# Compressed path's copies in single steps, the window keys' splits behind its hidden layer, early rotations two steps later, priority for two sums of every group

## The chip, the core and the metric

The kernel runs on one core of a Trainium2 chip. The core has five engines that run side by side, each with an instruction queue of its own: TensorE (PE in the profile; its weight loads are PEld), VectorE (DVE), ScalarE (ACT), GpSimd (POOL) and SyncE (SP), which here only issues transfers. Work passes between two on-chip memories, SBUF and PSUM (where matmuls accumulate, in banks of 512 float32 columns), and DRAM. The metric is the device time of one execution in microseconds, the median over several runs.

## What is computed

One layer of a decoder trunk on 512 tokens of width 1024. A wide projection feeds two token mixers: a causal pooling mixer over four window sizes, and sparse attention with 16 heads in 2 key groups and three branches (compressed keys, selected blocks, sliding window). With 512 tokens all blocks are selected and the window covers everything, so that two branches are plain causal attention with keys and values of their own. Two gates merge the mixers, an output projection and a residual follow, then a squared-ReLU MLP (1024 to 4096 to 1024), a residual and a norm. Cut to what matters here:

```python
h = rms_norm(x, norm_mix)
u, q, kc, vc, ks, vs, kw, vw, g_nsa, g_merge = split(h @ w_in)
q, ks, kw = apply_rope(q), apply_rope(ks), apply_rope(kw)
k_cmp = apply_rope(compress(kc, pe_k, w_ck1, w_ck2))
v_cmp = compress(vc, pe_v, w_cv1, w_cv2)
# compress: blocks of 32 tokens, every 16, plus pe; gelu(flat @ w1) @ w2
o = g0 * attend(q, k_cmp, v_cmp) + g1 * attend(q, ks, vs) + g2 * attend(q, kw, vw)
merged = sigmoid(g_a) * (pool_mixer(u) @ w_proj_pool) + sigmoid(g_b) * (o @ w_proj_nsa)
x = x + merged @ w_out
x = x + square(relu(rms_norm(x, norm_mlp) @ w_ff1)) @ w_ff2
out = rms_norm(x, norm_final)
```

## The kernel before

**Split products.** Every float32 matrix is held as a high and a low part (type fp32r in the profile). ScalarE copies the raw matrix into the high part, VectorE subtracts that from the raw matrix for the low part. A product is three matmuls: high by high, high by low, low by high. So each weight, once its transfer has landed, takes a ScalarE copy (line 475, or 366 in the MLP) and a VectorE subtraction (478, or 371) before TensorE can use it. The weight's name in the profile is `raw`, then `wh` and `wl` (`w3h` and `w3l`, `wkt`).

**Order.** The program is emitted in one order by Python code; a planner then sets the order of each engine's queue, with durations of its own. Of the instructions that it reckons ready at a moment, it takes the one emitted first. `tc.high_priority(n)` counts an instruction as emitted n places earlier. `behind(x)` keeps an instruction behind x on its engine. On the chip each engine follows its queue in the planned order; `raw` buffers, weight slots and PSUM banks are reused in turn.

**Steps.** TensorE's work is the backbone: `for k in P1` in the first phase goes through the columns of the input projection in the order `ck ks u0 wk0 u1 wk1 u2 wk2 kw wk3 cv V0 V1 V2 wv0 u3 wv1 q0 ...`, ending with `q2 pp0 pp1 pp2 pp3`. Each key's matmuls come in pieces. After each piece stand `ahead()`, which emits the next half of the next weight's two copies where a slot is free, and one yield. At each yield `run` calls `step_side`, which lets every generator in the queue `side` go on by one step. These side generators hold what follows a product on the other engines:

- `cmp_first` (line 893): copies the projection of the compressed keys or values (`ck`, `cv`) into an interleaved table on ScalarE (896, 897, twice each), adds the position rows (904) and makes the split table `cA` (907, 908). It is a plain function, called at the end of `cv`.
- `cmp_mlp1` (923) multiplies `cA` with the first compress weights. `cmp_rest` follows: gelu by a tanh (934 to 943), some empty steps, two transposes on TensorE (957), the copy `cg` on ScalarE with 60 places of priority (960), and the second weights on TensorE (969).
- `rope` (810): ScalarE takes the product out of PSUM (816), four transfers of 64 KB exchange the halves (`rs<-rx`, 819), then come empty steps, four products (836), two sums (829), one step each, and then `done`. In the attention phase the products run on GpSimd instead, in given places.
- `k_done` (849): splits rotated keys into `KH` and `KL` for each key group, four copies and two more on ScalarE (855, 859), two subtractions on VectorE (857). `k_done(0)` belongs to `ks`, `k_done(1)` to `kw`. `q_done` (865) does it for a pair of heads (867 to 871).
- `project_v` (the keys V0, V1, V2) multiplies the value and gate columns into four banks `psV`, in three pieces of the depth, four token tiles each; when it is done, ScalarE and VectorE copy the four banks out (1048 to 1050).
- `token_sums`, `pool_mix` and others run beside these.

**Groups.** The gate of mixer A, and the MLP's first layer, are computed with seven products in place of eight (Strassen's scheme): class `Group`, order A11, S3, S1, S2, A12, A22, S4 (the first MLP chunk in another order). `main` makes the combinations on VectorE: `u2 = s - b` (610), `u3 = c + u2` (611), `u3 = d + u3` (614). A22 goes on accumulating in the bank of c, which 611 must have read. Line 611's instruction is `roots`, behind which every weight subtraction of line 371 that is emitted later is kept.

Of the kernel before, what the change touches and what calls it, by code (L numbers as in the profile page):

```python
# [62 lines left out]
def trunk(ctx: ExitStack, tc: tile.TileContext, A, out):  # L63
# [507 lines left out]
    class Group:  # L571
# [29 lines left out]
        def main(self):  # L601
            while "A11" not in self.done:
                yield
            ACT.activation(self.s, self.ps["a"], AF.Copy)
            self.done.add("s")
            while not {"S1", "S2", "S3"} <= self.done:
                yield
            yield
            with tc.high_priority(60) if self.key[0] == "G" else nullcontext():
                DVE.tensor_tensor(self.u2, self.s, self.ps["b"], op=ALU.subtract)  # L610
                roots[:] = [DVE.tensor_tensor(self.u3, self.ps["c"], self.u2, op=ALU.add)]
            self.done.add("u3")
            yield
            DVE.tensor_tensor(self.u3, self.ps["d"], self.u3, op=ALU.add)
            self.done.add("u2")
            yield from self.act(self.u3, 1, 1)
# [107 lines left out]
    def behind(made):  # L724
        return tc.issue_after(made.ins)
# [3 lines left out]
    def sums0(i):  # L729
        junk = p0.tile([128, D], F32, tag="junk", bufs=1, name="junk")  # L730
        ACT.activation(junk, xt[i], AF.Square, accum_out=rr[i][:, 0:1])
        r = ACT.activation(rr[i][:, 1:2], rr[i][:, 0:1], AF.Sqrt, bias=eps_t, scale=1.0 / D)
        DVE.reciprocal(rr[i][:, 2:3], rr[i][:, 1:2])
        for h in range(2):
            c = slice(512 * h, 512 * h + 512)
            v = DVE.scalar_tensor_tensor(xt[i][:, c], xt[i][:, c], rr[i][:, 2:3], psg[h], op0=ALU.mult, op1=ALU.mult)
        return r, v
# [9 lines left out]
    def evac0(i, after=None):  # L747
        sl = slice(128 * i, 128 * i + 128)
        for a in range(2):
            ks = slice(4 * a, 4 * a + 4)  # L750
            r = ACT.activation(hT[0][:, ks, sl], trs[i][a], AF.Copy)
            with behind(after) if after else nullcontext():
                v = DVE.tensor_tensor(hT[1][:, ks, sl], trs[i][a], hT[0][:, ks, sl].bitcast(F32), op=ALU.subtract)
        for a in range(2 if i > 1 else 0):
            c = 128 * (i - 2)
            ACT.activation(quarter(MAf, 2 * a + 1)[:, :, c:c + 128], trs[i][a], AF.Copy)
        return r, v
# [8 lines left out]
    r, _ = evac0(1)  # L766
    with behind(r):
        r, _ = sums0(2)
# [4 lines left out]
    with behind(conv[0]):  # L773
        r, v = sums0(3)
    mode["first"] = None
    first_posts = []
# [29 lines left out]
    scored = {"pairs": 0, "rope": 0}  # L806
# [3 lines left out]
    def rope(ps, scale, done, after=0):  # L810

        assert not scored["rope"]
        scored["rope"] = 1
        xr = ap.tile([128, S], F32, tag="rx", bufs=1, name="rx")
        sw = ap.tile([128, S], F32, tag="rs", bufs=1, name="rs")
        ACT.activation(xr, ps, AF.Copy, scale=scale)
        for b in range(4):
            a = b ^ 1
            nc.sync.dma_start(sw[32 * b:32 * b + 32, :], xr[32 * a:32 * a + 32, :])
        yield  # L820
        eng = POOL if mode["pool"] else DVE
        hs = [slice(0, S // 2), slice(S // 2, S)]
        in_slots = mode["pool"]
        for _ in range(4 if in_slots else 2):
            yield

        def add(c):
            with behind(slot["low"]) if in_slots else nullcontext():
                DVE.tensor_tensor(xr[:, c], xr[:, c], sw[:, c], op=ALU.add)

        for c in hs:
            for t, table in ((xr, cosT), (sw, sinT)):
                while in_slots and not slot["long"]:
                    yield
                with behind(slot["scaled"]) if in_slots else nullcontext():
                    eng.tensor_tensor(t[:, c], t[:, c], table[:, c], op=ALU.mult)
                yield
            if c is hs[0]:
                continue
            add(hs[0])  # L840
            yield
            add(hs[1])
        while scored["pairs"] < after:
            yield
        for _ in done(xr):
            yield
        scored["rope"] = 0

    def k_done(br):
        def done(k):  # L850
            for g in range(2):
                r = [slice(64 * h, 64 * h + 64) for h in range(2)]
                src = k[r[g], :].rearrange("p (a b) -> p a b", a=4)
                for h in range(2):
                    ACT.activation(KH[g][r[h], :, br, :], src, AF.Copy)
                yield
                DVE.tensor_tensor(KL[g][r[g], :, br, :], src, KH[g][r[g], :, br, :].bitcast(F32), op=ALU.subtract)
                yield
                ACT.activation(KL[g][r[1 - g], :, br, :], KL[g][r[g], :, br, :].bitcast(F32), AF.Copy)
        return done  # L860
# [14 lines left out]
    with ExitStack() as c1:  # L875
# [15 lines left out]
        def cmp_first(kv):  # L891

            def post(ps):
                kc = scratch[:, 0:1024].rearrange("p (g t) -> p g t", g=2)
                for g in range(2):
                    ACT.activation(kc[0:64, g, :], ps[64 * g:64 * g + 64, :], AF.Copy)
                    ACT.activation(kc[64:128, g, 0:S - 1], ps[64 * g:64 * g + 64, 1:S], AF.Copy)
                a = scratch[:, 1024:2048].rearrange("p (j n) -> p j n", j=16)
                POOL.memset(a[:, :, 31:64:32], 0.0)
                o = 0 if kv == "k" else 16  # L900
                for g in range(2):
                    v = bass.AP(tensor=kc.tensor, offset=kc[:, g, :].offset,
                                ap=[list(kc.ap[0]), [2, 16], [16, 31]])
                    DVE.tensor_tensor(a[:, :, 32 * g:32 * g + 31], v,
                                      pec[:, o:o + 16, None].to_broadcast([128, 16, 31]), op=ALU.add)
                t = p1.tile([128, 16, 128], FR, tag="cA", bufs=1, name="cA")
                DVE.tensor_copy(t[:, :, 0:64], a)
                cA_low.append(DVE.tensor_tensor(t[:, :, 64:128], a, t[:, :, 0:64].bitcast(F32), op=ALU.subtract))
                cA[kv] = t
            return post  # L910

        cA, cA_low = {}, []
# [3 lines left out]
        def cmp_mlp1(kv, i):  # L916
            if i == 0:
                cps[kv] = ps1.tile([128, 256], F32, tag="V", bufs=4, name="psC1")
            ps = cps[kv]
            wH, wL = use(f"w{kv}{i}")  # L920
            for k in range(4):
                for w in (wH, wL):
                    PE.matmul(ps, cA[kv][:, 4 * i + k, :], w[:, k, :], start=i == 0 and k == 0 and w is wH,  # L923
                              stop=i == 3 and k == 3 and w is wL, skip_group_check=True)
            ahead()
            yield
            ahead()
            if i == 3:
                side.append(cmp_rest(kv, ps))

        def cmp_rest(kv, ps):
# [26 lines left out]
            gt = p1.tile([128, 2, 64], F32, tag="cg", bufs=2, name="cg")  # L958
            with tc.high_priority(60):
                ACT.activation(gt, pt, AF.Copy, scale=0.5)  # L960
            yield
            yield
            pm = ps1.tile([128, 2, 64], F32, tag="M", bufs=2, name="psM")
# [148 lines left out]
        def gates(g):  # L1112
# [5 lines left out]
            own = [pair(gate_f[0], i) for i in range(4)]  # L1118
            return Group(f"G{g}", sums_of.get, lambda: ps1.tile([128, S], F32, tag="V", bufs=4, name="psV"), own, act)

        first_posts += [cmp_first("k"), lambda ps: rope(ps, -0.125, k_done(0))]
        pr = ps1.tile([128, 36], F32, tag="M", bufs=2, name="psM")
        PE.transpose(pr, rows, ident[0:36, 0:36])
        DVE.tensor_copy(pec, pr)
# [55 lines left out]
    with ExitStack() as c2:  # L1180
# [304 lines left out]
        ps = ps2.tile([128, S], F32, tag="T", bufs=T_BANKS, name="psT")  # L1485
# [489 lines left out]
    ps = whole.ps["d"][0]  # L1975
# [13 lines left out]
    ps = whole.ps["d"][1]  # L1989
# [27 lines left out]
```

## Time and profile before

| | |
|---|---|
| median of 3 runs | 776.96 us (776.59 to 777.86) |
| the profiled execution | 777.74 us |
| its span, first to last instruction | 775.9 us |
| matmuls (PE instructions) | 4675 |
| DMA moved | 146.55 MB |

The span runs in four parts: the projections and the mixers' inputs up to about 165 us, attention to about 370, the output projections to about 440, and the MLP. Times in a timeline count from the start of the span. In a row of the timeline stand the start, the length, the engine, the line in the kernel, the operation, what is written and read with its shape, the count of merged instructions, and in brackets how long the engine was idle before it and what ended that. In the list of waits stand who waited for whom, the total, the count and the longest, in us. The releaser is inferred, and where an instruction waits for several things it is the one that came last by the profile.

### The profile page before, as it was taken

What the parts mean: (1) busy time and instruction counts of PE and PEld (TensorE: products, weight loads), DVE (VectorE), ACT (ScalarE), POOL (GpSimd) and SP (SyncE); (2) the same over time, 40 slices, a digit from 0 to 9 for tenths busy, and PEclk for the clock granted to TensorE, in tenths of its full rate; (3) what the DMA queues carried; (4) which work ended last, traced back from release to release, by engine and by line L of the source; (5) the groups of instructions that cost most, each with busy time, mean ns of one, the idle gap of its engine ahead of it and who ended that gap; (6) DMA issues with size and microseconds to landing.
All of it is one profiled execution on the core that took longest, in us unless ns stands there. A gap on an engine that the chain in (4) does not pass through costs nothing.

```text
span 775.9 us, 13217 instructions
## 1 busy us (share of the span) xinstructions
PE 759.2 (98%) x4675; PEld 673.5 (87%) x4675; DVE 657.2 (85%) x1267; ACT 507.7 (65%) x977; POOL 179.5 (23%) x261
## 2 busy tenths in 40 slices
PE   8999999999999999999999999999999999999996
PEld 6888889878888888888889899988998899889985
DVE  6898958467989989989689779997899779978997
ACT  6677635237978888899646476854774477437764
POOL 4000011115646766665000110111111111111101
PEclk9999999999999999999999999999999999999999
DMA  9553885974041933181357975989997999999952
GB/s 303 144 160 95 224 184 136 231 194 145 15 123 55 199 60 69 34 139 42 131 171 224 335 123 165 286 212 288 315 266 222 281 299 270 232 300 298 283 192 109
DMA packets 117708, 146.55 MB, mean 189 GB/s; under 512 B 5653, under 2 KB 90169, under 8 KB 117434
## 3 DMA queue, kind: packets, MB, share of 16 engines
q1 hardware_dynamic: 97658, 120.28, 47.7%
q0 software_dynamic: 19696, 24.64, 21.2%
q10 hardware_dynamic: 288, 0.79, 0.3%
q8 instruction: 37, 0.61, 0.3%
q14 instruction: 29, 0.24, 0.1%
HBM read 140.97 MB, written 51.38 MB: 248 GB/s over the span
## 4 chain that ended last, share of the span: by engine, by line
PE 81%; DVE 10%; ACT 4%; issue 3%; DMA 1%; POOL 0%; SPq 0%; DVEq 0%; ACTq 0%; POOLq 0%
PE psB L589 20%; PE psF L519 18%; PE psB L1631 15%; PE psB L519 6%; PE psS L1310 4%; PE psT L1372 4%; PE psO L1406 3%; PE psB L1579 3%; PE psV L589 3%; PE psF L651 1%; PE psC L923 1%; ACT P L1342 1%; DVE PT L1388 1%; DVE wl L478 1%; DVE P L1332 1%
## 5 line engine op out<-in xcount | busy, mean ns | idle before, releaser
L519 PE MATMUL psF<-R,wh 128*128 128x512 f32 x448 | 144.4, 399 | 0.0
L319 POOL DMA_DIRECT2D S<-w_ff x44 | 49.1, 1115 | 358.3 <-DMA S<-w_ff 295.3
L366 ACT ACTIVATE wh<-raw 128x1024 fp32r<-128x1024 f32 x73 | 77.0, 1057 | 67.9 <-PE psB L589 22.9
L1355 POOL TENSOR_SCALAR P<-P,sm,GT 128x128 f32<-128x128 f32 (+3 forms) x128 | 85.2, 716 | 68.5 <-DVE sm L1352 35.7
L371 DVE TENSOR_TENSOR wl<-raw,wh 128x1024 fp32r<-128x1024 f32 x73 | 88.8, 1219 | 14.2 <-ACT wh L366 14.0
L519 PEld LDWEIGHTS psF<-R,wh 128*128 128x128 f32 x448 | 80.5, 188 | 13.7
L519 PE MATMUL psF<-R,wl 128*128 128x512 f32 x224 | 88.1, 393 | 0.0
L475 ACT ACTIVATE wh<-raw 128x512 fp32r<-128x512 f32 (+1 forms) x84 | 50.2, 618 | 54.4 <-PE psF L519 27.8
L1342 ACT ACTIVATE P<-P,sm 128x128 f32<-128x128 f32 (+3 forms) x128 | 71.0, 557 | 9.8 <-DVE sm L1332 6.2
L478 DVE TENSOR_TENSOR wl<-raw,wh 128x512 fp32r<-128x512 f32 (+1 forms) x82 | 57.0, 703 | 21.4 <-ACT wh L475 21.1
L366 ACT ACTIVATE w3h<-raw 128x1024 fp32r<-128x1024 f32 x37 | 39.1, 1057 | 38.4 <-PE psB L589 14.1
L1332 DVE CUSTOM_DVE_ANT_0 P<-psS,cst 128x128 f32<-128x128 f32 (+3 forms) x128 | 59.3, 482 | 4.9 <-PE psT L1372 3.6
L589 PE MATMUL psB<-R,wh 128*128 128x256 f32 x336 | 60.0, 279 | 0.0
L1388 DVE TENSOR_TENSOR PT<-psT,PT 128x512 fp32r<-128x512 f32 (+2 forms) x96 | 56.2, 591 | 2.3 <-ACT PT L1383 2.0
L1383 ACT ACTIVATE PT<-psT 128x512 fp32r<-128x512 f32 (+2 forms) x96 | 49.0, 519 | 12.0 <-PE psT L1372 10.8
L371 DVE TENSOR_TENSOR w3l<-raw,w3h 128x1024 fp32r<-128x1024 f32 x37 | 45.1, 1220 | 10.3 <-ACT w3h L366 10.0
L589 PEld LDWEIGHTS psB<-R,wh 128*128 128x128 f32 x336 | 51.4, 188 | 0.2
L1372 PE MATMUL psT<-ident,P 128*128 128x128 f32 x320 | 50.3, 273 | 1.0 <-DVE PT L1388 0.5
L519 PEld LDWEIGHTS psF<-R,wl 128*128 128x128 f32 x224 | 42.1, 188 | 8.7
L1406 PE MATMUL psO<-PT,VV 128*128 128x256 f32 x320 | 48.5, 286 | 0.0
L1372 PEld LDWEIGHTS psT<-ident,P 128*128 128x128 f32 x320 | 39.6, 140 | 10.1 <-issue 1.4
L589 PE MATMUL psB<-R,wl 128*128 128x256 f32 x168 | 46.8, 279 | 0.0
(430 smaller groups left out, 2154.1 us busy)
## 6 DMA issues: line engine op xcount, KB each, us to landing
raw<-w_ff SPq DMA_DIRECT2D x54, 512.0 KB, 6.9
S<-w_ff POOLq DMA_DIRECT2D x44, 512.0 KB, 9.0
raw<-S SPq DMA_DIRECT2D x44, 512.0 KB, 6.6
raw<-w_in SPq DMA_DIRECT2D x32, 512.0 KB, 4.5
S<-w_ff SPq DMA_DIRECT2D x32, 512.0 KB, 6.5
S<-S SPq DMA_DIRECT2D x12, 512.0 KB, 7.2
raw<-w_proj_nsa SPq DMA_DIRECT2D x8, 512.0 KB, 3.9
x<-x SPq DMA_DIRECT2D x7, 512.0 KB, 6.2
```

The source lines that it names most:

```text
L366: ACT.activation(h, t, AF.Copy)
L371: DVE.tensor_tensor(l, t, h.bitcast(F32), op=ALU.subtract)
L478: eng.tensor_tensor(l[:, sl], t[:, sl], h[:, sl].bitcast(F32), op=ALU.subtract)
L519: PE.matmul(ps, a, b, start=first and j == 0, stop=last and j == n - 1, skip_group_check=True)
L589: PE.matmul(out, w[u][:, k, 128 * f:128 * f + 128], moving[v][:, k, :], **kw)
L1332: DVE.tensor_tensor_reduce(out=P[:, o:o + n].rearrange("p (a c) -> p a c", c=128), in0=s, in1=m, scale=1.0, scalar=3e38, op0=ALU.add, op1= ...
L1342: last_exp[:] = [ACT.activation(c, c, AF.Exp, bias=sm[:, 0, e:e + 1], scale=-1.0, accum_out=sm[:, 1, e:e + 1])]
L1355: r = POOL.tensor_scalar(P[:, o:o + n], P[:, o:o + n], sm[:, 2, e:e + 1], GT[:, qb, c + e:c + e + 1], op0=ALU.mult, op1=ALU.mult)
L1372: PE.transpose(pt[:, 128 * j:128 * j + 128], P[:, 128 * j:128 * j + 128], ident)
L1388: return DVE.tensor_tensor(dL, src, dH.bitcast(F32), op=ALU.subtract)
L1406: PE.matmul(ps[:, qb % 2, :, :], VV[:, k, b, g, :], t[:, j, :, :], start=False, stop=last and j == len(kbs) - 1 and t is tL, skip_group_ch ...
L1631: PE.matmul(ps[f], self.Y.of(y)[u][:, 2 * g + k, 128 * f:128 * f + 128], w[v][:, k, :], start=first and g == k == u == v == 0, stop=g == k ...
```

## The change

The edits, none of which adds or removes an instruction:

- The high priority of `u2` and `u3` in `Group.main`, so far only in the gate's group, holds in the MLP's eight groups too.
- `rope` lets four steps go by ahead of its products in the first phase, in place of two. (The attention phase already has four.)
- `k_done(1)` goes on only once the flag `gt` is set, which `cmp_rest` does right after it emits `cg`.
- `cmp_first` becomes a generator. For `cv` each of the four ScalarE copies is emitted in a step of its own; what follows the copies goes with the last. For `ck` it is run to its end at once, as before.

```diff
@@ class Group, main
-            with tc.high_priority(60) if self.key[0] == "G" else nullcontext():
+            with tc.high_priority(60):
                 DVE.tensor_tensor(self.u2, self.s, self.ps["b"], op=ALU.subtract)
                 roots[:] = [DVE.tensor_tensor(self.u3, self.ps["c"], self.u2, op=ALU.add)]
@@ rope
-        for _ in range(4 if in_slots else 2):
+        for _ in range(4):
             yield
@@ k_done
         def done(k):
+            while br and "gt" not in scored:
+                yield
             for g in range(2):
@@ cmp_first
                 for g in range(2):
+                    if kv == "v":
+                        yield
                     ACT.activation(kc[0:64, g, :], ps[64 * g:64 * g + 64, :], AF.Copy)
+                    if kv == "v":
+                        yield
                     ACT.activation(kc[64:128, g, 0:S - 1], ps[64 * g:64 * g + 64, 1:S], AF.Copy)
...
                 cA[kv] = t
+                yield
             return post
@@ cmp_rest
             with tc.high_priority(60):
                 ACT.activation(gt, pt, AF.Copy, scale=0.5)
+            scored["gt"] = True
@@ first phase
-        first_posts += [cmp_first("k"), lambda ps: rope(ps, -0.125, k_done(0))]
+        first_posts += [lambda ps: list(cmp_first("k")(ps)).clear(), lambda ps: rope(ps, -0.125, k_done(0))]
```

## The prediction

> **What bounds the kernel now.** I read the page first, then the busy time by stretch, then TensorE's waits, then the timeline of one engine at a time around each wait.
>
> ```profile
> span 775.9 us, 13217 instructions
> PE 759.2 (98%) x4675; PEld 673.5 (87%) x4675; DVE 657.2 (85%) x1267; ACT 507.7 (65%) x977; POOL 179.5 (23%) x261
> ...
> 20.00:60.00 40.00, 39.76 (x222) 34.63 (x221) 36.59 (x69) 27.11 (x49) 0.16 (x1) 1.00 0.52 144
> 80.00:140.00 60.00, 60.00 (x359) 53.06 (x358) 46.79 (x76) 30.84 (x49) 6.20 (x8) 1.00 0.74 188
> ...
> 620.00:640.00 20.00, 18.91 (x163) 18.74 (x162) 15.54 (x18) 13.57 (x20) 2.31 (x2) 1.00 1.06 296
> ...
> PE psB L589 <- ACT wh L366: 1.1, 1, 1.1
> PE psF L519 <- DVE wl L478: 1.0, 1, 1.0
> PE psM L969 <- ACT cg L960: 0.9, 1, 0.9
> PE psV L519 <- DVE wl L478: 0.8, 1, 0.8
> ...
> 31.94 5.46 PE psF L519 x24
> ```
>
> TensorE (PE) bounds it: busy 759.2 of 775.9 us, and the change adds and removes no matmul. Only TensorE's 16.7 us of idle time can change. The stretches give start and end, length, the busy time of PE, PEld, DVE, ACT and POOL, then granted clock, DMA share and GB/s: from 20 to 60 and from 80 to 140 TensorE is full. The list of waits names what the change can reach: four single waits of about 1 us. A wait costs more than its printed idle time, since matmuls overlap, so I count from when the next matmul was due. The chain's row gives the pace: 24 matmuls of 512 columns in 5.46, 0.228 each, so 0.135 for 304 columns and 0.114 for 256.
>
> **The change part by part.** Only the order changes. A planner orders each engine's instructions before the run: of those that it reckons ready, the one emitted first. A yield moves emission by a step; high_priority(60) puts an instruction 60 places ahead. The chip then keeps that order even where the head isn't ready.
>
> *The compressed path's copies in single steps (wait A).*
>
> ```profile
> 56.95 0.59 ACT L896 ACTIVATE scratch<-psF 64x512 f32<-64x512 f32 x1
> 61.24 1.40 ACT L475 ACTIVATE wh<-raw 128x608 fp32r<-128x608 f32 x3
> 62.44 0.77 DVE L478 TENSOR_TENSOR wl<-raw,wh 128x608 fp32r<-128x608 f32 x1
> 61.75 0.67 PE L519 MATMUL psV<-wh,R 128*128 128x304 f32 x2
> 63.27 0.41 PE L519 MATMUL psV<-wl,R 128*128 128x304 f32 x1 [0.85 <-DVE wl L478]
> ```
>
> After the two matmuls at 61.75 the next was due at 62.02 and came at 63.27: 1.25 lost. It waited for the low part of V1's second piece (128x608), whose high part stood behind cv's four copies, which hold ScalarE's order from 56.95 to 61.24. So far cv's copies and their VectorE work are emitted at once, and V1's two pieces in the first two steps of V0. Now it goes piece one, copy one, piece two, copy two. The second high part then follows at 56.95 + 0.59 = 57.54 and takes some 0.7; its low part (0.77) ends near 59, or 60 if VectorE is taken, and is due at 62.02. That is minus 1.25 us. The price: cv's last copy and its table come up to three steps later, each of nine matmuls, 9 x 0.135 = 1.2, so 3.6. The table was complete at 64.08 + 1.21 = 65.29 (first row of the next fence); 68.9 is still ahead of its first use, 73.68 there. Bounds: 0 if the planner leaves the copies first, minus 1.25 if not; I take minus 1.25.
>
> *The window keys' splits behind the transposed scores of the compressed path (wait B).*
>
> ```profile
> 64.08 1.21 DVE L908 TENSOR_TENSOR cA<-scratch,cA 128x1024 fp32r<-128x1024 f32 x1
> ...
> 65.66 1.93 ACT L855 ACTIVATE KH<-rx 64x512 fp32r<-64x512 f32 x3 [3.01 <-DVE rx L829]
> 69.62 0.63 ACT L859 ACTIVATE KL<-KL 64x512 fp32r<-64x512 f32 x1 [0.76 <-DVE KL L857]
> 70.28 1.15 ACT L475 ACTIVATE wh<-raw 128x512 fp32r<-128x512 f32 x2
> 71.62 0.66 ACT L1048 ACTIVATE VV<-psV 128x256 fp32r<-128x256 f32 x2
> 72.60 0.21 ACT L1050 ACTIVATE GT<-psV 128x48 f32<-128x48 f32 x1 [0.32 <-DVE VV L1049]
> ...
> 68.79 0.33 PE L957 MATMUL psM<-ident,ea 64*128 64x64 f32 x2
> 70.69 0.30 PE L519 MATMUL psV<-wh,R 128*128 128x304 f32 x1
> 71.87 0.29 PE L969 MATMUL psM<-cg,w2d 128*128 128x64 f32 x1 [0.89 <-ACT cg L960]
> 73.68 1.09 PE L923 MATMUL psC<-wkt,cA 128*128 128x256 f32 x8
> ```
>
> The matmul due at 70.69 + 0.135 = 70.83 came at 71.87: 1.04 lost. Its operand cg can be copied once the transposes end, at 69.12; ScalarE's order held the last key split until 70.25 (0.76 of it idle, for VectorE) and two weight pieces until 71.43. Now the six splits on ScalarE (6 x 0.64 = 3.8 us) are emitted after cg, which keeps its 60 places, and u3's two weight pieces too come ahead of them. Some splits will still run early, since the planner fills idle time and ScalarE sat idle for 3.01 before 65.66; what counts is that no chain of them is left between 69.12 and cg. Minus 1.04 us. Queued behind the splits are V's copies. The matmul at 73.68 needs the bank that they read first; with A and B gone it is due 2.29 earlier, at 71.4. If all six splits came between cg (68.3 by then) and those copies: 68.3 + 3.8 + 1.2 (71.62 to 72.81, the first bank's copies) = 73.3, 1.9 lost. Bounds minus 1.04 to plus 0.9; I take minus 1.04, by the row of 3.01, in which most splits find room.
>
> *Rotations two steps later (wait C).*
>
> ```profile
> 150.26 1.15 ACT L475 ACTIVATE wh<-raw 128x512 fp32r<-128x512 f32 x2 [3.75 <-PE psF L519]
> ...
> L819 SPq DMA_DIRECT2D rs<-rx x4: 529/588/601, 146.0 to 147.9; - x4
> DMA to landing us min/median/max: 5.2/5.7/6.0
> ...
> 153.28 0.42 DVE L836 TENSOR_TENSOR rx<-rx,cst 128x256 f32<-128x256 f32 x1 [2.10 <-DMA rs<-rx]
> 155.29 0.68 DVE L478 TENSOR_TENSOR wl<-raw,wh 128x512 fp32r<-128x512 f32 x1
> 157.99 0.69 DVE L478 TENSOR_TENSOR wl<-raw,wh 128x512 fp32r<-128x512 f32 x1
> ...
> 157.10 0.61 PE L519 MATMUL psF<-yd,wh 128*128 128x512 f32 x2
> 158.74 0.50 PE L519 MATMUL psF<-yd,wl 128*128 128x512 f32 x1 [1.02 <-DVE wl L478]
> ```
>
> Due at 157.10 + 2 x 0.228 = 157.56, come at 158.74: 1.18 lost. The operand is the second low part of pp2. Its high part was done at 151.41, but VectorE's head was the rotation of q2, idle 2.10 for four exchange transfers. In steps of emission: products 3 to 6, sums 7 and 8, pp2's first low part and q2's two low parts 9, pp2's second low part 10. Two steps on: products 5 to 8, then pp2's first low part, a sum, pp2's second low part, a sum, and q2's low parts in 11. Products and sums take (155.29 - 153.28) / 6 = 0.34. So from 153.28: four products to 154.6, one gate product (L1166, some 0.6), a low part 0.6, a sum 0.34, a low part 0.7: 156.9, or 157.2 behind the other sum; due 157.56. Minus 1.18, of which I leave 0.3 for so narrow a margin. If the transfers, with TensorE 2.29 ahead, land no earlier by the clock, the wait is 2.29 - 0.66 = 1.63 instead: plus 0.45. Bounds minus 1.18 to plus 0.45; the transfers are the same four, issued from the same place. The other early rotations (ks, kw, q0, q1) are covered: from 20 to 60 and from 80 to 140 TensorE idles 0.24 and 0.00, and VectorE has 3.4 and 13.2 us free. They cost nothing; without the cover one would cost its six instructions, 2.0 us.
>
> *Priority in the MLP's groups (wait D).*
>
> ```profile
> raw<-w_ff SPq DMA_DIRECT2D x54, 512.0 KB, 6.9
> ...
> L277 SPq DMA_DIRECT2D raw<-w_ff x1: 384/384/384, 610.5 to 610.5; - x1
> DMA to landing us min/median/max: 13.4/13.4/13.4
> ...
> 625.08 1.22 DVE L371 TENSOR_TENSOR w3l<-raw,w3h 128x1024 fp32r<-128x1024 f32 x1 [2.68 <-ACT w3h L366]
> 626.94 0.69 DVE L611 TENSOR_TENSOR MA<-psB,MA 128x512 f32<-128x512 f32 x1
> ...
> 626.41 0.28 PE L589 MATMUL psB<-R,wl 128*128 128x256 f32 x1
> 627.78 0.35 PE L589 MATMUL psB<-xT4H,w3h 128*128 128x256 f32 x1 [1.08 <-ACT wh L366]
> ```
>
> A22's first matmul was due at 626.52 and came at 627.78: 1.26 lost. It writes the bank that L611 reads, and L611 ended at 627.63, 0.15 before; so I take L611 for the releaser, not the copy named. L610 and L611 stood behind the low part at 625.08, which waited for its high part and that for a load of 13.4 us, issued at 610.5. Put ahead, in the idle 2.68, they would leave some 0.2 to wait: minus 1.05. But priority decides only among instructions that the planner reckons ready, and it has no reason to reckon this load late. Bounds 0 to minus 1.05; I take 0, the end that the present order is nearest to.
>
> The Trainium skill, "DMA: Bandwidth & Descriptors", section "Anatomy of one DMA", puts a transfer at about 2.0 us plus its bytes at 436 GB/s, an estimate of 3.2 us for 512 KB; by it no load here would be late, and rival 4 below would have no chance. The trace disagrees: median 6.9, here 13.4.
>
> The sum: -1.25 - 1.04 - 1.18 + 0.3 = -3.2. The profiled execution took 777.74 us around its span of 775.9, so it would take 774.6; the median of the runs lies 0.78 below it: **773.8 us**.
>
> **The rivals.**
> 1. *One of the three waits stays*, likeliest C with its margin of 0.3: 1.1 back, 774.9. For it: the planner doesn't know when a transfer lands. Against: the new order no longer hangs on it by the count above.
> 2. *D goes as well*: 773.8 - 1.05, 772.8. For it the idle 2.68; against it see D.
> 3. *The splits come in front of V's copies*: 1.9 back, 775.7. For it: they are now emitted just ahead of them. Against: the idle 3.01.
> 4. *The MLP's transfers set the end*: if the late load lands when it did, D grows by what was won, and all is given back: 776.9. For it the DMA share of 1.06 from 620 to 640; against it, D is the only wait of TensorE on psB in the list, so that only one load of the MLP came too late.
> 5. *Slower*: priority puts L610 and L611 ahead of the low part of A12's weight, which TensorE needs as S2 ends. VectorE then waits for S2, and A12 for all three: 0.7 + 0.7 + 1.2 = 2.6 us a group. The first such group leaves 0.6 of the gain, the second turns it: 773.8 + 5.2 = 779.0. It decides where that low part isn't done when S2 ends. For it: a load of 13.4. Against: no wait of A12 now.
>
> **How the numbers follow.** Forecast 0.44; rivals in order 0.15, 0.10, 0.10, 0.10, 0.11. A measurement tells about 0.2%, 1.6 us, from no change, so faster means under 775.4. Faster: 0.44 + 0.10 + 0.12 of rival 1 = 0.66; within: 0.03 + 0.10 + 0.10 = 0.23; slower: 0.11. The range, 772.3 to 777.0, holds the forecast (alone 773.0 to 774.6) and rivals 1 to 4, rival 4 up to its middle; it leaves out 0.16.
>
> **What would show it.** Right: no wait over 0.3 us at psV L519, psM L969 and psF L519; the high part of 128x608 on ScalarE behind the first copy of cv; cg within 0.7 us of its transposes; both low parts of pp2 ahead of those of q2. Wrong: a wait at psC L923 (rival 3), a longer one at A22 (4), one at A12 for its low part (5), or new waits in the attention stage, where a shifted start may change the planner's order though nothing there is edited.

## The result, and the profile after

| | before | after |
|---|---|---|
| median of six runs each, on one chip | 776.80 us (775.69 to 778.25) | 773.05 us (772.35 to 773.65) |
| ratio of the times, 95% interval | | 0.9950 (0.9937 to 0.9962) |
| profiled execution, its span | 777.74, 775.9 us | 773.65, 771.9 us |

The change takes 3.75 us off the median; the forecast was 773.8, the range 772.3 to 777.0. Compared once more, later, the same kernel gave 772.96 against 776.89, with the same ratio; one execution of the kernel before took 1530.72 us there and is left out of the ratio.

The page of the kernel after, its first lines:

```profile
span 771.9 us, 13216 instructions
PE 759.2 (98%) x4675; PEld 674.9 (87%) x4675; DVE 657.6 (85%) x1267; ACT 507.9 (66%) x977; POOL 179.5 (23%) x261
```

TensorE's work is the same 759.2 us; its idle time fell from 16.7 to 12.7. The busy time by stretch, in the columns of before (start and end, length, PE, PEld, DVE, ACT, POOL, clock, DMA share, GB/s), shows where:

```profile
60.00:80.00 20.00, 20.00 (x131) 18.65 (x130) 16.87 (x36) 14.71 (x32) 0.00 (x0) 1.00 0.53 143
...
140.00:160.00 20.00, 20.00 (x90) 16.56 (x89) 10.56 (x20) 5.91 (x11) 1.16 (x1) 1.00 0.77 160
...
620.00:640.00 20.00, 20.00 (x174) 20.00 (x173) 16.95 (x20) 14.13 (x20) 3.49 (x3) 1.00 1.09 290
```

TensorE is full in all three stretches, where it had worked 18.26, 18.98 and 18.91 (the first from the same view of before). Its list of waits (who waited for whom, total, count, longest) has none of the four left:

```profile
PE psM L722 <- DMA grow<-norm_mix: 2.3, 1, 2.3
PE psTr L744 <- issue: 1.4, 1, 1.4
PE psS L1318 <- DVE sm L1340: 0.8, 2, 0.5
PE psT L1380 <- DVE PT L1396: 0.5, 2, 0.4
...
PE psC L930 <- DVE cA L914: 0.2, 1, 0.2
```

**ScalarE around waits A and B** in the timeline of after (start, length, engine, line, operation, tiles, in brackets the idle time before and what ended it):

```profile
56.04 1.16 ACT L475 ACTIVATE wkt<-raw 128x512 fp32r<-128x512 f32 x2 [0.44 <-DMA raw<-w_cv]
...
58.55 0.59 ACT L900 ACTIVATE scratch<-psF 64x512 f32<-64x512 f32 x1
59.04 0.70 ACT L475 ACTIVATE wh<-raw 128x608 fp32r<-128x608 f32 x1
...
63.72 0.63 ACT L857 ACTIVATE KH<-rx 64x512 fp32r<-64x512 f32 x1 [2.13 <-DVE rx L829]
64.25 0.79 ACT L475 ACTIVATE wh<-raw 128x304 fp32r<-128x304 f32 x2
65.07 1.92 ACT L857 ACTIVATE KH<-rx 64x512 fp32r<-64x512 f32 x3
67.01 1.36 ACT L861 ACTIVATE KL<-KL 64x512 fp32r<-64x512 f32 x2
68.40 1.15 ACT L475 ACTIVATE wh<-raw 128x512 fp32r<-128x512 f32 x2
69.57 0.28 ACT L967 ACTIVATE cg<-psM 128x128 f32<-128x128 f32 x1
```

The transposes whose result cg copies, in TensorE's timeline of after:

```profile
68.05 0.33 PE L964 MATMUL psM<-ident,ea 64*128 64x64 f32 x2
```

A went as forecast: the 128x608 high part stands at 59.04, behind cv's first copy. B did not. All six key splits (KH x1, KH x3, KL x2) still run ahead of cg, and so do u3's two weight pieces (68.40). The chain is about as long as before; it only starts earlier, with KH at 63.72, 1.94 before the 65.66 of the kernel before. VectorE's side of wait C in after:

```profile
151.35 0.43 DVE L836 TENSOR_TENSOR rx<-rx,cst 128x256 f32<-128x256 f32 x1 [2.06 <-DMA rs<-rx]
...
152.70 0.68 DVE L478 TENSOR_TENSOR wl<-raw,wh 128x512 fp32r<-128x512 f32 x1
153.31 0.42 DVE L829 TENSOR_TENSOR rx<-rx,rs 128x256 f32<-128x256 f32 x1
153.64 0.68 DVE L1174 TENSOR_TENSOR MA<-psF,MA 128x512 f32<-128x512 f32 x1
154.24 0.68 DVE L478 TENSOR_TENSOR wl<-raw,wh 128x512 fp32r<-128x512 f32 x1
154.84 0.42 DVE L829 TENSOR_TENSOR rx<-rx,rs 128x256 f32<-128x256 f32 x1
```

This is the order counted out in the prediction: four products, a low part, a sum, a gate product, the second low part. And wait D, in the transfers of after from 607.5 to 608.5 (the issue of one 512 KB load, then its landing):

```profile
DMA to landing us min/median/max: 9.3/9.3/9.3
```

The load that took 13.4 us in the profiled execution of before took 9.3 here. VectorE's order there is the one of before: the traces of before and of the kernel with the priority edit alone have the same instruction list on every engine. So D's going needs another reason than the edit; the next section has it.

### The profile page after: what moved, and what is told of

Read it like the earlier page. It is cut to its first block, busy times and chain, and to the rows that moved or that the text cites. A ratio compares the mean times of both kernels' runs of the same rounds, so it can differ in the third digit from the quotient of the medians.

```text
span 771.9 us, 13216 instructions
## 1 busy us (share of the span) xinstructions
PE 759.2 (98%) x4675; PEld 674.9 (87%) x4675; DVE 657.6 (85%) x1267; ACT 507.9 (66%) x977; POOL 179.5 (23%) x261
## 4 chain that ended last, share of the span: by engine, by line
PE 86%; DVE 8%; ACT 3%; issue 2%; POOL 0%; DMA 0%; DVEq 0%; ACTq 0%; POOLq 0%
PE psF L519 21%; PE psB L589 20%; PE psB L1639 15%; PE psB L519 6%; PE psS L1318 4%; PE psT L1380 4%; PE psO L1414 3%; PE psB L1587 3%; PE psV L589 3%; PE psV L519 2%; PE psF L651 1%; PE psC L930 1%; ACT P L1350 1%; DVE PT L1396 1%; DVE P L1340 1%
```

## The experiments

Printed waits overlap with matmuls in flight, and starts differ from one execution to the next, so I count in one ledger. Each matmul of a kernel is matched with the same one of the kernel before, and the starts are subtracted, each counted from its span's start. "Start" is the median of these shifts over matmuls from 30 to 50 us of before. "A+B" is the change of that median from there to 85 to 110, "C" from there to 161 to 175, "D" from 590 to 618 to 640 to 700. Minus is time won against the profiled execution of before. "Landed" is the longest of the four transfers that q2's rotation waits for, from issue to landing, by the view of transfers from 140 to 160. What is not in a column (165 to 600 and the end) came to 0.6 us at most. Each ratio is against executions of the kernel before on the same chip; the medians of different rows come from different chips.

```
kernel               start   A+B     C      D    span   landed | median (runs)  ratio, 95%
before                0.00   0.00   0.00   0.00  775.9    6.0  |
before, second look   0.01  -0.35   0.39  -1.33  774.7    6.6  | 776.42 (1)
only_priority         0.16   0.06   1.95  -1.33  776.9    7.6  | 776.61 (10)  0.9999 0.9989-1.0009
only_copies          -0.35  -1.38   1.73  -1.33  774.6    7.5  | 775.47 (10)  0.9985 0.9975-0.9996
only_keys             0.32  -0.08   0.77  -1.33  775.8    6.3  | 776.39 (10)  0.9995 0.9985-1.0004
only_rotations        0.28  -0.35  -1.38  -1.33  773.3    6.7  | 775.07 (10)  0.9977 0.9968-0.9986
only_rotation_q2     -0.83   0.00  -0.69  -1.33  773.2    7.2  | 774.51 (10)  0.9981 0.9970-0.9991
only_rotation_kw      0.32   0.11   0.63  -1.33  776.3    6.2  | 776.98 (10)  1.0001 0.9989-1.0012
without_keys         -0.66  -1.77  -0.03  -1.33  772.2    8.3  | 773.12 (4)   0.9954 0.9937-0.9972
without_copies       -0.46  -0.41  -1.33  -1.33  772.4    5.8  | 774.22 (8)   0.9975 0.9964-0.9986
without_rotations    -0.20  -1.60  -0.62  -1.33  772.3    5.9  | 774.08 (7)   0.9971 0.9959-0.9983
after                 0.61  -2.47  -1.36  -1.33  771.9    5.8  | 773.05 (6)   0.9950 0.9937-0.9962
after, second look   -0.28  -1.81  -1.33  -1.33  771.2    5.6  | 772.96 (5)   0.9950 0.9937-0.9962
q2_four_steps_more   -0.06  -1.53  -1.26  -1.33  771.8    7.4  | 773.10 (5)   0.9951 0.9939-0.9964
```

Three things can be read off it at once. **Four rows are one program**: before, its second look, only_priority and only_keys have the same list of instructions on every engine in their traces, so that what they differ by, 0.4 us in A+B and 1.95 in C, is the execution and not the order. **D is one execution's**: thirteen of the fourteen profiles lack it, whatever their order. **C is not one number**: among kernels with q2's rotation where it was, it runs from -0.62 to 1.95, and is largest where the transfers landed last (1.73 and 1.95 at 7.5 and 7.6 us).

### Each edit alone

**The priority in the MLP's groups alone**

```diff
-            with tc.high_priority(60) if self.key[0] == "G" else nullcontext():
+            with tc.high_priority(60):
```

> The kernel before plus the priority edit alone. Laid side by side, the planned order of every engine's instructions is the same as before, so theory 1 (the edit is empty) expects the time of before within 0.1%, and the waits at 62, 71 and 157 us as before. It also gives a second look at the wait at A22: theory 1a (that wait comes with this order of transfers) expects it again, 1.0 to 1.4 us; theory 1b (it is an accident of one execution) expects a load of A22 that lands in 7 to 9 us and no wait. A rival in which priority matters on the chip would show L610 ahead of the low part at 625.

Measured: 776.61, ratio 0.9999 (0.9989 to 1.0009); no difference. D is gone from this profile although no engine's order changed. And C grew, in TensorE's timeline of this kernel:

```profile
158.20 0.50 PE L519 MATMUL psF<-yd,wl 128*128 128x512 f32 x1 [1.65 <-DVE wl L478]
160.91 0.50 PE L519 MATMUL psF<-yd,wl 128*128 128x512 f32 x1 [1.05 <-DVE wl L478]
```

Here both of pp2's low parts came late, the first by 1.65: the last of the four transfers had taken 7.6 us, and VectorE's head stood idle 4.05 (this kernel's VectorE):

```profile
155.44 0.43 DVE L836 TENSOR_TENSOR rx<-rx,cst 128x256 f32<-128x256 f32 x1 [4.05 <-DMA rs<-rx]
```

So one profile had sized C at 1.18, near the lower end of what the old order loses.

**The copies in single steps alone**

```diff
                 for g in range(2):
+                    if kv == "v":
+                        yield
                     ACT.activation(kc[0:64, g, :], ps[64 * g:64 * g + 64, :], AF.Copy)
+                    if kv == "v":
+                        yield
...
                 cA[kv] = t
+                yield
```

> The kernel before plus the copies in single steps alone. Theory 1 (one edit, one wait): the wait at psV L519 (62 us) is gone, minus 1.2 us; the waits at psM L969 and psF L519 stay at 0.9 and 1.0 of idle, shifted by 1.2. Rival (the edits only work together): the low part of 128x608 stays late because the rotation's products still stand in front of it on VectorE, and 0.5 us or more of the wait remains.

Measured: 775.47, ratio 0.9985 (0.9975 to 0.9996). The wait at 62 went (A), and the one at psM too, but a new one came at V2's low part. TensorE, and ScalarE ahead of it, in this kernel:

```profile
67.28 0.41 PE L519 MATMUL psV<-wl,R 128*128 128x304 f32 x1 [0.81 <-DVE wl L478]
```

```profile
61.86 2.58 ACT L855 ACTIVATE KH<-rx 64x512 fp32r<-64x512 f32 x4 [0.30 <-DVE rx L829]
64.46 0.46 ACT L475 ACTIVATE wh<-raw 128x304 fp32r<-128x304 f32 x1
...
65.59 0.46 ACT L475 ACTIVATE wh<-raw 128x304 fp32r<-128x304 f32 x1
```

With the copies out of the way the key splits run 3.8 us earlier by the clock (KH at 61.86, before at 65.66) and now stand in front of V2's two pieces. Of the 2.29 that A and B cost, 1.38 is won.

**The keys' splits behind cg alone**

```diff
         def done(k):
+            while br and "gt" not in scored:
+                yield
...
+            scored["gt"] = True
```

> The kernel before plus the keys' splits behind cg alone. Theory 1: the wait at psM L969 is gone, minus 1.0 us, cg starts within 0.7 us of its transposes; the other two waits stay. Rival: the planner fills ScalarE's idle time with the splits as before, four or more of the six still stand ahead of cg, and 0.5 us or more of that wait remains. Second rival (V's copies): a wait of up to 1.9 us at psC in the first wv0 product.

Measured: 776.39, ratio 0.9995 (0.9985 to 1.0004); A+B -0.08. ScalarE of this kernel:

```profile
65.88 1.93 ACT L857 ACTIVATE KH<-rx 64x512 fp32r<-64x512 f32 x3 [3.02 <-DVE rx L829]
67.82 0.63 ACT L861 ACTIVATE KL<-KL 64x512 fp32r<-64x512 f32 x1
68.46 0.63 ACT L857 ACTIVATE KH<-rx 64x512 fp32r<-64x512 f32 x1
69.84 0.63 ACT L861 ACTIVATE KL<-KL 64x512 fp32r<-64x512 f32 x1 [0.76 <-DVE KL L859]
70.50 1.15 ACT L475 ACTIVATE wh<-raw 128x512 fp32r<-128x512 f32 x2
71.68 0.28 ACT L962 ACTIVATE cg<-psM 128x128 f32<-128x128 f32 x1
```

Split for split this is the order of before, and so are the lists of the other engines. The splits are emitted behind cg and still stand ahead of it in the list; even cg at a priority of 400 places, which was planned but not run, changes no engine's list. So emission and priority do not decide here: it looks as if the planner has the splits ready, and ScalarE idle, before it has cg ready. This is where step B of the prediction fails.

**The rotations two steps later alone**

```diff
-        for _ in range(4 if in_slots else 2):
+        for _ in range(4):
             yield
```

> The kernel before plus the rotations two steps later alone. Theory 1: at pp2 the low parts stand ahead of q2's two low parts, the wait at psF L519 (157 us) is gone, minus 1.2 us; the waits at 62 and 71 us stay. Rival: the wait went only because TensorE's earlier start shifted it against the four exchange transfers; then alone, without that shift, 0.5 us or more of the wait remains.

Measured: 775.07, ratio 0.9977 (0.9968 to 0.9986). C is gone (-1.38) with the last transfer at 6.7. The waits of A and B only trade places: 1.44 at 63.91, in front of 0.16 at psM, and -0.35 for both together.

### One edit left out, and q2's rotation alone

The next three kernels are the kernel after with the lines of one edit, as the three diffs above have them, put back to before.

> The changed kernel with the keys' splits back where they were (copies in single steps and later rotations stay). Theory 2, after the runs of single edits: the keys' edit doesn't clear the wait at psM L969, it only lets V2's two weight pieces pass the window keys' copies on ScalarE; without it a wait of 0.5 to 0.9 us at psV L519 near 67 us comes, as with the copies alone, and psM stays clear: 0.5 to 0.9 us above the changed kernel. Rival (the prediction): without it psM L969 waits 0.9 again. Third: the later rotation does the same work, no wait at all, time within 0.1% of the changed kernel.

Without the keys' edit: 773.12, ratio 0.9954 (0.9937 to 0.9972), against 0.9950 with it. A+B is -1.77, beside -2.47, -1.81 and -1.53 of the three profiles that have the edit. Its worth lies inside what differs between executions. There is no wait at V2's pieces, and psM waits 0.5, where the theory had nothing and its rival 0.9. C is back with 0.84 in TensorE's timeline of this kernel:

```profile
154.75 0.50 PE L519 MATMUL psF<-yd,wl 128*128 128x512 f32 x1 [0.84 <-DVE wl L478]
```

The four transfers had taken up to 8.3 us: the later rotation gives the low parts a fixed head start, and transfers late enough use it up. In this execution nothing of C was won (-0.03).

> The changed kernel with cv's copies emitted at once again. Theory 2: the wait at psV L519 near 62 us is back with 1.2 to 1.4 us of idle, psM L969 waits at most 0.3, psF L519 is clear: 1.3 us above the changed kernel. Rival: the keys' edit with the later rotation keeps ScalarE free and the wait is under 0.7.

Without the copies' edit: 774.22, ratio 0.9975 (0.9964 to 0.9986), A+B -0.41 with 1.4 waited at psV.

> The changed kernel with the early rotations two steps earlier again. Theory 2: psV L519 and psM L969 stay clear (copies and keys do that), and the wait at psF L519 near 155 us is back with 1.0 to 2.7 us of idle, by how late the four exchange transfers land: 1.0 to 2.7 us above the changed kernel. Rival: the rotation of kw is needed near 62 to 70 us as well, and one of psV and psM waits 0.5 us or more.

Without the later rotations: 774.08, ratio 0.9971 (0.9959 to 0.9983), A+B -1.60 with 0.6 waited at V2's low part, as with the copies alone, so the rival came. psF waited only 0.4, less than the theory had it, with transfers that landed within 5.9 us. Against the whole change (0.9950) the copies are worth 0.0025, 1.9 us, and the rotations 0.0021, 1.6 us, each give or take some 1.3 (an estimate from the two intervals).

> The kernel before, with the rotation of q2 alone two steps later (those of ks, kw, q0, q1 as before). Theory 2: the wait at psF L519 near 157 us is gone, by this one rotation; the waits at psV L519 and psM L969 stay at 0.8 to 0.9, since it was kw's rotation that brought psM down to 0.2 in the run of all rotations. Rival: psM is at 0.2 here too, by chance of the planner.

```diff
+    turns = [0]
...
+        turns[0] += 1
-        for _ in range(4 if in_slots else 2):
+        for _ in range(4 if in_slots or turns[0] == 5 else 2):
```

With the fifth rotation, q2's, two steps later and no other: 774.51, ratio 0.9981 (0.9970 to 0.9991), beside 0.9977 with all. C is q2's. A+B stands at 0.00, psM and psV wait 0.9 each.

### What was left: D, the window keys' rotation, and a residue

> The kernel before, unchanged, profiled once more. Theory (wait D was an accident of one execution): no wait of over 0.3 us on psB at L589 near 627, the 512 KB load of w_ff that is issued near 610.5 lands in under 10 us, and the span is about 1.2 us shorter than 775.9 on this account, 774.3 to 776.0 with the 0.6 by which starts differ. Rival (D belongs to the order): the wait of about 1.1 us on psB is there again. In both cases the waits at psV (0.7 to 0.9 printed), psM (0.8 to 1.0) and psF (1 to 2.7, the more the later the exchange transfers land) are there, since they come from the order.

Measured: span 774.7, the load that is issued at 610.5 landed after 9.6 us, and A22's first matmul came on time. VectorE in the second look at the kernel before:

```profile
622.30 1.22 DVE L371 TENSOR_TENSOR w3l<-raw,w3h 128x1024 fp32r<-128x1024 f32 x1
...
624.69 0.69 DVE L611 TENSOR_TENSOR MA<-psB,MA 128x512 f32<-128x512 f32 x1
```

The same low part that started at 625.08 in the first look starts at 622.30 here, directly behind the instruction ahead of it in the queue (line 380, 621.16 to 622.39). The order is unchanged and only the load's landing differs, so D was that one load.

> The kernel before with the rotation of the window keys alone two steps later, all other rotations as they were. Theory (the wait at psM is one of ScalarE's order, and the key splits move behind it only when their sums do): in the order written, cg now stands between the two weight pieces instead of behind both, so the wait at psM falls from 0.9 to 0.1 to 0.3, the wait at psV at 62 stays or grows (0.8 to 1.5), and the wait at psF stays (1 to 2.7). Time 0.3 to 1.0 us under the kernel before: 775.2 to 776.4. Rival (the earlier rotations do nothing, only q2's counts): 776.2 to 777.0 with psM at 0.9.

```diff
-        for _ in range(4 if in_slots else 2):
+        for _ in range(4 if in_slots or scored["turn"] == 2 else 2):
```

My theory that the window keys' rotation cures B fell. 776.98, ratio 1.0001 (0.9989 to 1.0012). ScalarE of this kernel, and TensorE:

```profile
66.60 1.93 ACT L855 ACTIVATE KH<-rx 64x512 fp32r<-64x512 f32 x3 [3.17 <-DVE rx L829]
...
71.22 0.63 ACT L475 ACTIVATE wh<-raw 128x512 fp32r<-128x512 f32 x1
71.87 0.28 ACT L960 ACTIVATE cg<-psM 128x128 f32<-128x128 f32 x1
```

```profile
69.34 0.33 PE L957 MATMUL psM<-ident,ea 64*128 64x64 f32 x2
72.29 1.08 PE L969 MATMUL psM<-cg,w2d 128*128 128x64 f32 x8 [0.75 <-ACT cg L960]
```

cg does stand between the two weight pieces, but the whole chain began at 66.60, 0.94 later than before (0.62 when counted from TensorE's start), since the keys' sums come later now. So the place of cg in the list doesn't decide B alone; when the chain ahead of it begins counts as much here. In only_rotations psM waited little because TensorE had already waited 1.44 for V1.

> The kernel after, unchanged, to stand beside the next kernel on the same chip and to show how its waits differ between executions. Theory: 772.4 to 773.7; no wait at psV near 62 or at psM near 71, whatever the transfers do; at psF none if q2's four exchange transfers land within 7 us of their issue, and 0.5 to 1.0 if they take over 7.5. Rival (the psF wait is gone for good): none there even with landings over 7.5.

Measured: 772.96; nothing at psV or psF, the transfers landed within 5.6 us, so the case over 7.5 did not come up. But psM waits 0.43, where the profile above had none. ScalarE and TensorE in this second look at the kernel after:

```profile
55.84 1.16 ACT L475 ACTIVATE wkt<-raw 128x512 fp32r<-128x512 f32 x2 [1.13 <-DMA raw<-w_cv]
...
69.36 0.28 ACT L967 ACTIVATE cg<-psM 128x128 f32<-128x128 f32 x1
```

```profile
67.16 0.33 PE L964 MATMUL psM<-ident,ea 64*128 64x64 f32 x2
69.78 1.08 PE L977 MATMUL psM<-cg,w2d 128*128 128x64 f32 x8 [0.43 <-ACT cg L967]
```

cg comes 13.52 us behind the copy of w_cv's weight here, and 69.57 - 56.04 = 13.53 in the first look. So the whole chain hangs on when that 512 KB load lands (after 4.2 us in the first look, 4.9 here). Counted from TensorE's start (the column start), the copy began at 56.04 - 0.61 = 55.43 in the first look and at 55.84 + 0.28 = 56.12 in the second: 0.69 later, and A+B is 0.66 less.

> The kernel after with the rotation of q2 alone emitted another four steps later (8 instead of 4). In the order written, pp2's two low parts stand ahead of all and of all but one of the four products, instead of behind all four. Theory (psF waits only where pp2's second low part stands behind products that wait for the transfers): no wait over 0.3 at psF near 155 whatever the landing; the time is that of the kernel after or up to 0.5 us less, 772.0 to 773.5, since the kernel after waits there only in some executions. Rival (a later q2 is paid for at the heads that follow): a new wait of 0.5 to 1.5 us on psS or psT after 158, and 773.5 to 774.5.

```diff
-        in_slots = mode["pool"]
-        for _ in range(4):
+        in_slots, scored["turn"] = mode["pool"], scored["turn"] + 1
+        for _ in range(8 if scored["turn"] == 5 else 4):
```

Measured: 773.10, ratio 0.9951 (0.9939 to 0.9964), the time of the kernel after. psF has no wait with transfers of up to 7.4 us, where the four-step order of only_rotation_q2 had kept 0.64 of C at 7.2 (-0.69 beside -1.33). No new wait came behind it. ScalarE and TensorE of this kernel show the residue of B once more:

```profile
56.34 1.16 ACT L475 ACTIVATE wkt<-raw 128x512 fp32r<-128x512 f32 x2 [1.44 <-DMA raw<-w_cv]
...
69.86 0.28 ACT L967 ACTIVATE cg<-psM 128x128 f32<-128x128 f32 x1
```

```profile
70.28 1.08 PE L977 MATMUL psM<-cg,w2d 128*128 128x64 f32 x8 [0.70 <-ACT cg L967]
```

Again 13.52 us lie between the two; the copy is at 56.34 + 0.06 = 56.40 by TensorE's start, 0.97 later than in the first look, and A+B is 0.94 less. Three profiles agree to 0.03 us.

The load of w_cv is not only late by chance. The kernel before issues it at 50.04 (its SyncE), the second look at the kernel after at 50.9, which is 51.1 by TensorE's start:

```profile
50.04 0.37 SPq L277 DMA_DIRECT2D raw<-w_cv  x1
```

```profile
L277 SPq DMA_DIRECT2D raw<-w_cv x1: 368/368/368, 50.9 to 50.9; - x1
```

By that count it is issued at 51.1 to 51.2 in all six profiles with all rotations later, and at 50.0 to 50.1 in the eight others, those with kw's or q2's rotation alone among them. It goes out as VectorE ends a low part of w_in's weight (49.97 in the kernel before, 50.83 in the second look at the kernel after), so that VectorE's order sets it. Of the rotations that moved, those of q0 and q1 come later than this moment; so by elimination it is the rotation of ks that delays the load, by 1.1 us. That is more than the 0.66 and 0.94 by which A+B falls short of the first look. A kernel with ks's rotation alone later, or with it alone left where it was, was not run.

## Why the prediction was right, and where it was not

- **The total.** Forecast -3.2, medians -3.75 (interval of the ratio: -2.95 to -4.9). The likeliest case came, with no wait in either profile of the kernel after at the places of A and C. But the terms were not all right: B came out some 0.35 smaller than forecast and C some 1.1 to 1.3 larger, and the two errors go against each other. The profiled executions differ by 4.09, but 1.33 of that is D, which is no gain of the change, and 0.61 went the other way at the start of the span.
- **A: right, mechanism and size.** -1.25 was forecast. In the profile of after the shift goes from 0.61 at the start to -0.73 behind psV, 1.34. The pieces stand as forecast, 1.5 us later by the clock (59.04 for 57.54), with time to spare before their use. The prediction left out what the copies alone show: the splits move up too and delay V2's pieces by 0.8. In the whole change the later rotation keeps them back (KH at 63.72, in only_copies 61.86), so this price was not paid.
- **B: size near, reason wrong.** The step that failed is "what counts is that no chain of them is left between 69.12 and cg", that is, that emitting the splits after cg would clear ScalarE ahead of it. All six splits and u3's two pieces still run ahead of cg, which comes 1.19 us behind its transposes in the profile of after (69.57 against 68.05 + 0.33), not within 0.7. The keys' edit alone moves nothing, and with the other two it is not to be told from none (0.9950 and 0.9954). B shrinks because the chain begins earlier once cv's copies no longer stand in one block on ScalarE: by TensorE's start KH comes at 65.7 in before and without_copies, at 62.2 in only_copies and at 63.1 in after. That the term for B came near its size is luck: the gain was booked under the edit for the keys and comes from the one for the copies. A+B came to -2.47, -1.81 and -1.53, on average -1.94, where -2.29 was forecast: some 0.35 of B stays, by the landing of the load of w_cv. The idle 3.01 did speak rightly against rival 3: psC waits 0.2, as in the kernel before.
- **C: mechanism right, size too small.** The order came out as counted, and C is won by q2's rotation alone. The margin of 0.3 was not needed in the two profiles of after. And 1.18 was one execution's loss. Over the six other profiles that kept the old place of q2's rotation, column C lies on average at (0.39 + 1.95 + 1.73 + 0.77 + 0.63 - 0.62) / 6 = 0.81, so that the old order lost about 2.0 to 2.2, and the new one none at landings up to 6.7. With -1.94 for A and B and -2.0 to -2.2 for C, where these landings are common, the sum is about -4.0; so a C that was sized too small is enough for a median that outran the forecast; but -3.2 lies inside the interval of the medians, so that this excess is not shown by them. The other rotations were put at nothing because TensorE and VectorE had room. By the elimination above ks's is not free: the load of w_cv goes out 1.1 us later with it, and the rest of B starts there.
- **D: right for the edit, wrong for the profile.** Taking 0 for the priority was right, and the unchanged lists agree with the reason given, that the planner does not reckon this load late. But the prediction treated D as a part of the kernel before. It belongs to one execution.
- **The rivals.** Rival 1, as C, did not come in a profile of the kernel after, but its ground is real: transfers of 8.3 us brought C back with 0.84 in without_keys, whose rotations are those of after. Rival 2's wait was gone, but by that execution's load and not by the edit. Rival 3 had no trace, rival 4 fell with D, and rival 5 could not come, since priority moved nothing.

The Trainium skill, "DMA: Bandwidth & Descriptors", section "Anatomy of one DMA", gives 2.0 us plus the bytes at 436 GB/s for transfers that GpSimd issues, an estimate of 2.2 us for one of 64 KB. The transfers here are issued by SyncE. Near 51 us the fourteen profiles have 2.2 to 4.6 us for such transfers, near the estimate at the shortest; near 145 us the same kind took 4.0 to 8.3, and there the measurement decides.

## What to carry to other kernels

Before a wait is charged to the code, look at a second profile of the same kernel: a wait behind a load may be that execution's (D), or change several times over with the landing (C: 0.6 to 3.1 us lost in one and the same place). A later place in the emission order need not move an instruction back: the key splits kept their place on ScalarE, which had been idle for 3.02 us ahead of them. And a wait that is cured can hand its time to the next one in line (the copies alone cleared waits of 2.29 and won 1.38), so edits are to be measured one at a time and one left out.

## What the runs showed of the hardware

The four transfers of 64 KB ahead of q2's rotation, issued from the same place of the program, had the last of them landed between 5.6 and 8.3 us after its issue over fourteen profiles, and one 512 KB load of w_ff took 13.4 us once and 9.0 to 10.0 in the thirteen other profiles. The granted clock was 0.997 to 0.999 in all of them and plays no part. The first matmul waited between 2.3 and 3.5 us for its load, and TensorE's start at 30 to 50 us moved over 1.4 us (-0.83 to 0.61): as much as one of the edits brings.
